# A new hand-written step order in four layers, and 46 products moved from GpSimd to VectorE

## The chip, the cores and the metric

The kernel runs on one core of a Trainium2 chip. The core has five engines that run their own instruction queues: TensorE (PE in the rows; PEld is its loading of weights), VectorE (DVE), ScalarE (ACT), GpSimd (POOL) and SyncE (SP, which here issues the loads from memory). The metric is the device time of one launch in microseconds (us).

## What is computed

A transformer of two blocks in float32, on 256 positions of 1024 features. The first block has an even layer (three kinds of gated attention on compressed, selected and windowed keys, plus differential attention) and an odd layer (block attention of 16 heads), each followed by an MLP. The second block has two equal layers without an MLP; each mixes three branches, gates them and projects the result:

```python
for layer in range(DEPTH):                    # second block, DEPTH = 2
    h = rms_norm_2(x, norm_g[layer])
    cols = split_columns(h @ w_in[layer])
    y_gdn = gdn_branch(cols, ...)             # gated delta rule, both directions, chunks of 64
    y_mla = mla_branch(cols, positions, ...)  # latent attention, 6 heads
    y_rwkv = rwkv7_branch(cols, ...)          # RWKV-7 recurrence, both directions
    mix = jnp.concatenate([y_gdn, y_mla, y_rwkv], axis=-1) * jax.nn.silu(cols['gate'])
    x = x + mix @ w_out[layer]
return rms_norm_2(x, final_norm_g)
```

Inside `gdn_branch`, with `cum` the running sum of the log decay of a chunk:

```python
d_incl = jnp.exp(jnp.where(incl, cum[..., :, None] - cum[..., None, :], -jnp.inf))
a_mat = beta[..., :, None] * jnp.einsum('nhcid,nhcjd->nhcij', k, k) * d_strict
sol = lax.linalg.triangular_solve(a_mat, rhs, lower=True, unit_diagonal=True)
```

## The kernel before

The program is first recorded and then laid out. Every operation of a layer is noted in a list (class `Order`), with the tiles that it reads and writes; when the list is complete, `Order.plan` lays it out once, at build time, into one fixed instruction list for each engine. It takes at each moment the ready operation with the smallest number in the list, within a window of 600 entries, and gives tiles their places in four arenas: `sb` (working tiles), `wt` (raw weights), `fr` (split weights and activations) and `ps` (PSUM banks). All instructions are issued by one helper, so they all carry line 614, `put`; rows are told apart by engine, operation, tile and shape.

Each layer is cut into parts, and each part into steps (a generator that yields after each). A string, `ORDER`, names one step after the other:

```python
def weave(self, order):
    for word in order.split():
        n, _, steps = word.partition("*")
        ...
        for _ in range(int(steps or 1)):
            if self.step(parts[n]):
                ended.add(n)
```

So `ORDER` sets the numbers in the list, and with them the priorities and, where several operations are ready, the order of the instructions on each engine.

A product with weights is done in three matmuls on split numbers (`mm3`): ScalarE copies the raw weights to the rounded type (the CAST `fr<-wt`), VectorE subtracts that copy from the raw weights (the weight subtraction, TENSOR_TENSOR `fr<-wt,fr`, most of them 128x1024), and TensorE multiplies high and low parts. Matmuls with output 128x512 on `fr` tiles are called wide below. A matmul on `sb` tiles in plain float32 stands as one row in the program's order and as two records in the trace.

The parts that matter here:

- Even layer E: `attn0` to `attn3`, `diff0`, `diff1` (differential attention), `cmpk` and `comp` (the compressed branch; its second step holds a softmax on VectorE and ScalarE, two transposes, and four products of 128x256), `out_a` (output projection of the first six feature tiles; needs `comp` and `diff0`), `out_b` (of the last two, 24 wide matmuls; needs `diff1`).
- Odd layer O: `proj0` to `proj3` (projections of four head groups), `attn0` to `attn3` (scores, softmax on ScalarE, transposes, products), `out_a`, `out_b`.
- A layer of the second block, S0 and S1: `gdn_proj`, `gdn_prep`, `gdn_inv` (the triangular inverse by small matmuls of 32x32 and 64x64), `gdn_uw`, `gdn_steps`, `gdn_end`; the same for `rwkv_proj`, `rwkv_prep`, `rwkv_inv`, `rwkv_mats`, `rwkv_steps` (the chain of 64x64 matmuls over the chunks), `rwkv_end`; `mla_proj`, `mla_attend`, `mla_end`; `gates` (column blocks of the gate projection); `out_a` (output projection of the feature tiles of gdn and mla), `out_b` (of rwkv's two tiles, 24 wide matmuls).

In `gdn_prep` (L1837) a copy of 128x48 takes the running sums out of PSUM, copies of 64x12 and 128x12 turn them round, and then 14 products of 128x384 on `gu`, `m`, `E` and `EN` (L1887 to L1906) and exponentials on ScalarE make the matrices to be inverted. In `gdn_end` two products of 128x384 (L2043) and in `rwkv_end` six of 128x256 and one of 128x512 (L2356 to L2363) make factors for the results. All these products name GpSimd as their engine; without a name `mul`, `add` and `sub` go to VectorE. GpSimd's other work is memsets, small DMAs of weights, `rstd_pool`, a product in `cmpk` and copies for `mla_proj`.

Of the kernel before, what the change touches and what calls it, by code (L numbers as in the profile page):

```python
# [1504 lines left out]
class Second(Layer):  # L1505
# [41 lines left out]
    def start(self):  # L1547
# [29 lines left out]
        "gdn_proj*10 rwkv_proj gdn_proj*4 rwkv_proj gdn_proj*2 rwkv_proj*2 gdn_prep*3 rwkv_proj gdn_prep*3 rwkv_proj "  # L1577
        "gdn_inv*2 rwkv_proj gdn_inv*2 rwkv_proj gdn_inv rwkv_proj*3 gdn_inv*6 rwkv_proj*2 gdn_inv*2 rwkv_proj "
        "gdn_inv*6 rwkv_proj gdn_inv*2 rwkv_proj gdn_inv rwkv_proj gdn_inv*3 rwkv_proj gdn_inv*5 rwkv_prep gdn_inv*3 "
        "rwkv_prep gdn_inv*6 rwkv_prep*4 gdn_inv gdn_uw rwkv_prep gdn_uw*3 rwkv_prep*2 gdn_uw*2 rwkv_inv*2 gdn_uw "  # L1580
        "rwkv_inv gdn_uw rwkv_inv*4 gdn_uw rwkv_inv gdn_uw rwkv_inv*11 gdn_uw rwkv_inv*2 gdn_steps rwkv_inv gdn_steps "
# [1033 lines left out]
```

## Time and profile before

| | |
|---|---|
| median of 3 runs | 1231.8 us (1231.16 to 1233.77) |
| the profiled execution | 1228.06 us |
| its span, first to last instruction | 1226.3 us |
| busy: TensorE | 1073.2 us (88% of the span) |
| busy: VectorE | 832.9 us (68%) |
| busy: ScalarE | 577.1 us (47%) |
| busy: GpSimd | 75.7 us (6%) |

The stages of the span, by the first and last instructions of their parts: E from 0 to 158.2, its MLP to 339.8, O to 460.0, its MLP to 641.7, S0 to 927.4, S1 to 1214.7, then the final norm. Busy is the time in which an engine executes an instruction; a share over the whole span mixes stages that have different limits.

### The profile page before, as it was taken

How to read it: one execution, taken by the hardware profiler on the slowest of the kernel's cores; microseconds unless marked ns; L12 is line 12 of the kernel's file. 1: busy time of each engine (PE TensorE's matmuls, PEld its weight loads, DVE VectorE, ACT ScalarE, POOL GpSimd, SP SyncE). 2: the span in 40 equal slices, each digit the busy share in tenths (PEclk: the TensorE clock that was granted, in tenths of full speed). 3: DMA queues.
4: the chain of work that ended last, by engine and by line, in shares of the span. 5: the costliest groups of instructions: out<-in, count | busy, mean ns of one | idle time of the engine just before them, and what ended most of it. 6: DMA issues, size and time to landing. Idle time of an engine off the chain costs nothing. (4 is left out here: it accounts for less than half of the span.)

```text
span 1226.3 us, 22320 instructions
## 1 busy us (share of the span) xinstructions
PE 1073.2 (88%) x8969; PEld 950.9 (78%) x8969; DVE 832.9 (68%) x1757; ACT 577.1 (47%) x1069; POOL 75.7 (6%) x150
## 2 busy tenths in 40 slices
PE   8999899999998999999997974489899895768895
PEld 7887699999897979999986873478568784657663
DVE  5556775545565566555488899962877889788445
ACT  4565454444436555444354543226564453332751
POOL 0000000000000000000001310002200310001200
PEclk9999899999998999999998885699899797678797
DMA  9930375565542454675671410142214342102110
GB/s 265 275 106 21 118 222 174 177 200 195 174 148 82 143 172 139 222 224 174 210 247 36 132 44 1 51 117 84 70 41 127 86 117 73 36 13 90 51 50 35
DMA packets 129682, 151.51 MB, mean 124 GB/s; under 512 B 15979, under 2 KB 111338, under 8 KB 129578
## 3 DMA queue, kind: packets, MB, share of 16 engines
q1 hardware_dynamic: 128745, 147.89, 38.7%
q0 software_dynamic: 832, 2.20, 0.7%
q8 instruction: 70, 1.15, 0.4%
q14 instruction: 35, 0.28, 0.1%
HBM read 147.42 MB, written 1.07 MB: 121 GB/s over the span
## 5 line engine op out<-in xcount | busy, mean ns | idle before, releaser
L614 PE MATMUL ps<-fr 128*128 128x256 f32 (+3 forms) x5112 | 788.1, 315 | 23.2 <-DVE fr L614 9.2
L614 PEld LDWEIGHTS ps<-fr 128*128 128x128 f32 (+1 forms) x5112 | 714.4, 194 | 83.6 <-DVE fr L614 14.4
L614 PE MATMUL ps<-sb 64*64 64x64 f32 (+14 forms) x3857 | 309.3, 286 | 118.3 <-DVE sb L614 83.3
L614 PEld LDWEIGHTS ps<-sb 64*64 64x64 f32 (+5 forms) x3857 | 241.1, 171 | 179.8 <-DVE sb L614 77.3
L614 DVE TENSOR_TENSOR fr<-wt,fr 128x1024 fp32r<-128x1024 f32 (+4 forms) x269 | 314.7, 1202 | 55.4 <-ACT fr L614 54.8
L614 ACT CAST fr<-wt 128x1024 fp32r<-128x1024 f32 (+4 forms) x269 | 263.0, 1022 | 80.7 <-DMA wt<-in_mlp_w 25.6
L614 ACT ACTIVATE sb<-sb 128x256 f32<-128x256 f32 (+8 forms) x347 | 163.3, 504 | 209.4 <-DVE sb L614 187.2
L614 DVE TENSOR_TENSOR sb<-ps,sb 128x256 f32<-128x256 f32 (+7 forms) x169 | 85.8, 517 | 171.5 <-ACT sb L614 90.0
L614 ACT ACTIVATE sb<-ps 128x384 f32<-128x384 f32 (+7 forms) x166 | 77.3, 475 | 228.2 <-PE ps L614 207.3
L614 DVE TENSOR_TENSOR sb<-sb 128x256 f32<-128x256 f32 (+24 forms) x436 | 146.1, 348 | 10.9 <-POOL sb L614 4.2
L614 DVE SCALAR_TENSOR_TENSOR sb<-sb 128x256 f32<-128x256 f32 (+8 forms) x228 | 88.8, 407 | 20.6 <-ACT sb L614 17.0
L614 DVE TENSOR_TENSOR sb<-sb,ps 128x512 f32<-128x512 f32 (+3 forms) x82 | 46.7, 582 | 31.9 <-PE ps L614 31.5
L614 POOL TENSOR_TENSOR sb<-sb 128x384 f32<-128x384 f32 (+4 forms) x55 | 52.8, 980 | 171.3 <-PE ps L614 97.3
L614 ACT ACTIVATE sb<-ps,sb 128x256 f32<-128x256 f32 (+3 forms) x70 | 34.8, 542 | 47.7 <-PE ps L614 45.7
L614 DVE TENSOR_TENSOR fr<-sb,fr 128x512 fp32r<-128x512 f32 (+1 forms) x38 | 24.7, 649 | 21.5 <-ACT fr L614 21.3
L614 ACT CAST fr<-sb 128x512 fp32r<-128x512 f32 x32 | 19.9, 621 | 32.4 <-DVE sb L614 32.4
L614 DVE COPY sb<-ps 128x384 f32<-128x384 f32 (+9 forms) x45 | 21.3, 478 | 19.7 <-PE ps L614 19.2
L614 POOL MEMSET sb<- 128x2 f32 (+3 forms) x59 | 5.7, 140 | 463.6 <-DVE sb L614 286.8
L614 DVE TENSOR_SCALAR sb<-sb 128x2 f32<-128x2 f32 (+15 forms) x119 | 26.2, 234 | 4.8 <-POOL sb L614 2.0
L614 DVE CUSTOM_DVE_ANT_0 sb<-ps,sb 128x128 f32<-128x128 f32 (+1 forms) x80 | 24.6, 352 | 6.7 <-PE ps L614 3.5
L614 POOL TENSOR_SCALAR sb<-sb 128x2 f32<-128x2 f32 (+1 forms) x8 | 2.5, 312 | 416.9 <-DVE sb L614 416.9
L614 ACT ACTIVATE fr<-ps,sb 128x256 fp32r<-128x256 f32 x52 | 19.8, 488 | 11.5 <-PE ps L614 10.8
(30 smaller groups left out, 162.8 us busy)
## 6 DMA issues: line engine op xcount, KB each, us to landing
wt<-in_mlp_w SPq DMA_DIRECT2D x128, 512.0 KB
wt<-in_w_in SPq DMA_DIRECT2D x38, 512.0 KB
wt<-in_od_w_in SPq DMA_DIRECT2D x24, 512.0 KB
wt<-in_w_out SPq DMA_DIRECT2D x16, 512.0 KB
wt<-in_ev_w_in SPq DMA_DIRECT2D x14, 512.0 KB
wt<-in_ev_w_in SPq DMA_DIRECT2D x16, 256.0 KB
wt<-in_ev_w_out SPq DMA_DIRECT2D x8, 512.0 KB
...
```

What stands on the lines that cost most here:

```text
L614: fn(*a, **k)
```

## The change

The strings `ORDER` of E, O, S0 and S1 are written anew; the steps and what they compute are the same, and each step is still named as often. In S0 and S1 the 46 products named above (23 in each layer) lose their engine's name and go to VectorE. The diff, with one line of each pair of strings; the strings go on behind the dots:

```diff
@@ class Even, ORDER @@
-        "dp1 attn1 dp1 cmpk dp1 attn2 dp0 cmpk diff1*2 dp0 attn1 attn3 diff1 attn3 diff1 attn1 diff1 attn3 diff1 cmpk "
-        "diff1*2 attn3 diff1 attn1 diff1 cmpk dp0 cmpk attn3 cmpk*2 dp0 cmpk comp dp0 out_b dp0 diff0 comp diff0*4 "
-        "out_b diff0*4 out_b diff0 comp out_a*10")
+        "attn1 diff1 cmpk*2 diff0 cmpk attn3 attn2 attn3 diff1 diff0 comp diff0*6 comp diff0 comp diff0 out_a out_b "
+        "out_a*3 out_b*2 out_a*6")
...
@@ class Odd, ORDER @@
-        "proj0*9 proj1*2 attn0 proj1*2 attn0 proj1 attn0 proj1*2 attn0 proj1*2 attn0 proj2 attn0 proj2 attn1 proj2*2 "
+        "proj1*6 proj0*6 proj2 proj0*3 proj1 attn0 proj1 proj2 attn0 proj2 proj3*2 proj1 proj2*3 proj3 attn1 proj3*3 "
...
@@ class Second, ORDER, second string (S1) @@
-        "mla_attend*2 rwkv_steps*2 mla_attend mla_end rwkv_steps mla_end rwkv_steps out_a*2 rwkv_end*2 out_a*3 "
-        "rwkv_end out_a*3 rwkv_end out_b*3 out_a*2")
+        "rwkv_steps*3 mla_attend*2 rwkv_end mla_attend*3 mla_end*2 rwkv_end out_a*3 rwkv_end out_a*3 rwkv_end out_b "
+        "out_a out_b*2 out_a*3")
...
@@ gdn_prep @@
-                self.mul(gu, b6(gd), bc6("inc" + "fb"[d]), nc.gpsimd)
+                self.mul(gu, b6(gd), bc6("inc" + "fb"[d]))
...
-                self.add(m, b6(cd), bc6("m" + "fb"[d]), nc.gpsimd)
+                self.add(m, b6(cd), bc6("m" + "fb"[d]))
...
-                    self.mul(E, E, b6(sb[:, t, 0]), nc.gpsimd)
+                    self.mul(E, E, b6(sb[:, t, 0]))
...
-                    self.sub(m, b6(cd), bc6("mn"), nc.gpsimd)
+                    self.sub(m, b6(cd), bc6("mn"))
...
-                    self.mul(EN, EN, b6(sb[:, t, 1]), nc.gpsimd)
+                    self.mul(EN, EN, b6(sb[:, t, 1]))
@@ gdn_end @@
-                     gr[:, None, None, :].to_broadcast([128, 3, 2, 64]), nc.gpsimd)
+                     gr[:, None, None, :].to_broadcast([128, 3, 2, 64]))
@@ rwkv_end @@
-            self.mul(G[:, t], sg[t], row("rwkv_ln_g_2"), nc.gpsimd)
+            self.mul(G[:, t], sg[t], row("rwkv_ln_g_2"))
...
-            self.add(B[:, t], B[:, t], row("rwkv_ln_b_2"), nc.gpsimd)
-            self.mul(B[:, t], B[:, t], sg[t], nc.gpsimd)
+            self.add(B[:, t], B[:, t], row("rwkv_ln_b_2"))
+            self.mul(B[:, t], B[:, t], sg[t])
```

**Place 1: TensorE at the end of E.** Before, from the transposes of `out_b`'s input, the two of `comp`'s second step and three of `diff0` (the nine of 128x128), over `comp`'s four products (128x256) and three more of `diff0` to the 24 wide matmuls of `out_b`:

```order
L614 MATMUL ps<-sb 128x128 x9
L614 MATMUL ps<-sb 128x256 x4
L614 MATMUL ps<-sb 128x128 x3
L614 MATMUL ps<-fr 128x512 x24
L614 MATMUL ps<-sb 128x128 x3
```

And of the changed kernel, up to `comp`'s four products and what follows them:

```order
L614 MATMUL ps<-fr 128x512 x4
L614 MATMUL ps<-sb 128x128 x3
L614 MATMUL ps<-fr 128x512 x3
L614 MATMUL ps<-sb 128x128
L614 MATMUL ps<-fr 128x512 x2
L614 MATMUL ps<-sb 128x128 x2
L614 MATMUL ps<-fr 128x512
L614 MATMUL ps<-sb 128x128 x2
L614 MATMUL ps<-fr 128x512 x2
L614 MATMUL ps<-sb 128x128 x3
L614 MATMUL ps<-sb 128x256 x4
L614 MATMUL ps<-fr 128x512 x12
```

17 of `out_b`'s wide matmuls (these 12, and five in the rows just ahead) and the transposes of `diff0` have moved from behind `comp`'s products to ahead of them; the other 7 stand among the 12 behind them.

In O the same can be said in words: before, four groups of scores are followed directly by the first six transposes of `attn0`; now 72 matmuls of 128x256, which belong to `proj3`, stand between scores of `attn2` and those transposes.

**Place 2: the front of S1, VectorE and TensorE.** VectorE before, around the copy of 128x48 in `gdn_prep`:

```order
L614 SCALAR_TENSOR_TENSOR sb<-sb 128x24 x2
L614 COPY sb<-ps 128x48
L614 TENSOR_TENSOR sb<-sb 128x24
L614 COPY sb<-sb 64x2x6 x4
L614 COPY sb<-sb 128x12 x2
L614 TENSOR_TENSOR sb<-ps,sb 128x384
L614 TENSOR_TENSOR fr<-wt,fr 128x1024 x4
```

VectorE of the changed kernel there:

```order
L614 SCALAR_TENSOR_TENSOR sb<-sb 128x24 x2
L614 TENSOR_TENSOR sb<-sb 128x384 x4
L614 COPY sb<-ps 128x48
L614 TENSOR_TENSOR sb<-sb 128x24
L614 TENSOR_TENSOR sb<-sb 128x384
L614 COPY sb<-sb 64x2x6 x4
L614 COPY sb<-sb 128x12
L614 TENSOR_TENSOR sb<-sb 128x384
L614 COPY sb<-sb 128x12
L614 TENSOR_TENSOR sb<-ps,sb 128x384
L614 TENSOR_TENSOR fr<-wt,fr 128x1024 x4
```

Four of the moved products (`sb<-sb 128x384`) stand ahead of the 128x48 copy and two among the copies behind it; the other eight follow later. TensorE in the same layer, where the 32x32 matmuls of `gdn_inv`'s last stage stand, before:

```order
L614 MATMUL ps<-fr 128x256 x46
L614 MATMUL ps<-sb 32x32 x96
L614 MATMUL ps<-sb 128x128 x7
L614 MATMUL ps<-fr 128x256 x4
L614 MATMUL ps<-sb 64x64 x12
```

And of the changed kernel:

```order
L614 MATMUL ps<-fr 128x256 x48
L614 MATMUL ps<-sb 32x32 x48
L614 MATMUL ps<-sb 128x128 x4
L614 MATMUL ps<-sb 32x32 x48
L614 MATMUL ps<-sb 128x2 x4
L614 MATMUL ps<-sb 64x64 x152
```

The four of 128x128 that now stand between the two halves are `rwkv_prep`'s, which VectorE scales next; they were the first four of the seven behind all 96.

**Place 3: TensorE at the end of S1.** The last steps of `rwkv_steps` (64x64), the wide matmuls of `out_a`, the four transposes of `out_b`'s input (128x128) and its 24 wide matmuls, before:

```order
L614 MATMUL ps<-sb 64x256 x3
L614 MATMUL ps<-sb 64x64 x8
L614 MATMUL ps<-fr 128x512 x30
L614 MATMUL ps<-sb 64x64 x16
L614 MATMUL ps<-fr 128x512 x36
L614 MATMUL ps<-sb 128x128 x4
L614 MATMUL ps<-fr 128x512 x24
```

And of the changed kernel (`mla_attend`'s last products are the 64x256):

```order
L614 MATMUL ps<-sb 64x64 x8
L614 MATMUL ps<-sb 128x128 x4
L614 MATMUL ps<-sb 64x64 x8
L614 MATMUL ps<-sb 64x256 x4
L614 MATMUL ps<-fr 128x512 x51
L614 MATMUL ps<-sb 128x128
L614 MATMUL ps<-fr 128x512
L614 MATMUL ps<-sb 128x128 x3
L614 MATMUL ps<-fr 128x512 x38
```

The 30 wide matmuls have gone from the middle of the 64x64 chain to behind it, so that 51 instead of 36 stand between the chain and the transposes; 10 of `out_a` and the 24 of `out_b`, among the last 38 with four more, follow them.

## Rows read from the trace of the kernel before

**Rows 1.** The page: the span, and each engine's busy time, share and instructions.
```profile
span 1226.3 us, 22320 instructions
...
PE 1073.2 (88%) x8969; PEld 950.9 (78%) x8969; DVE 832.9 (68%) x1757; ACT 577.1 (47%) x1069; POOL 75.7 (6%) x150
```
**Rows 2.** Windows by stage: length, busy PE, PEld, DVE, ACT, POOL, clock, DMA share, GB/s.
```profile
0.00:158.20 158.20, 142.75 (x1041) 126.03 (x1042) 98.43 (x268) 85.90 (x209) 5.05 (x12) 0.95 0.55 162
339.80:460.00 120.20, 115.73 (x870) 104.66 (x869) 71.31 (x151) 67.02 (x151) 0.89 (x2) 0.97 0.40 132
...
641.70:927.40 285.70, 221.34 (x2366) 191.09 (x2365) 226.75 (x553) 129.44 (x253) 33.75 (x66) 0.83 0.24 69
927.40:1214.70 287.30, 230.23 (x2362) 197.17 (x2360) 217.95 (x536) 122.96 (x242) 32.32 (x47) 0.82 0.22 63
```
**Rows 3.** Windows of three stretches: the end of E, O, the front of S0.
```profile
118.00:134.00 16.00, 10.94 (x64) 8.80 (x65) 14.75 (x49) 9.43 (x27) 1.05 (x1) 0.57 0.40 129
380.00:390.00 10.00, 6.54 (x29) 4.76 (x29) 6.91 (x29) 9.91 (x31) 0.00 (x0) 0.66 0.43 136
720.00:800.00 80.00, 38.98 (x818) 35.99 (x818) 77.13 (x207) 25.45 (x41) 0.52 (x1) 0.62 0.13 35
```
**Rows 4.** Timeline of TensorE: start, length, what, [idle before it <-releaser].
```profile
127.08 1.33 PE L614 MATMUL ps<-sb 128*128 128x128 f32 x5 [3.95 <-DVE sb L614]
129.11 4.21 PE L614 MATMUL ps<-sb 128*128 128x256 f32 x10 [0.70 <-DVE sb L614]
...
383.54 5.37 PE L614 MATMUL ps<-sb 128*128 128x128 f32 x20 [3.43 <-ACT sb L614]
...
806.31 3.59 PE L614 MATMUL ps<-fr 128*128 128x320 f32 x13 [0.65 <-DVE sb L614]
...
1048.73 4.22 PE L614 MATMUL ps<-sb 32*32 32x32 f32 x57 [0.19 <-ACT sb L614]
...
1191.30 1.08 PE L614 MATMUL ps<-sb 128*64 128x64 f32 x16 [0.48 <-ACT sb L614]
...
1194.30 8.37 PE L614 MATMUL ps<-fr 128*128 128x512 f32 x34 [0.34 <-DVE fr L614]
1204.60 0.88 PE L614 MATMUL ps<-sb 128*128 128x128 f32 x4 [1.94 <-DVE sb L614]
1206.17 8.57 PE L614 MATMUL ps<-fr 128*128 128x512 f32 x24 [0.69 <-ACT fr L614]
```
**Rows 5.** Timeline of VectorE, behind the inversion in S1.
```profile
1052.36 0.87 DVE L614 SCALAR_TENSOR_TENSOR sb<-sb,ps 128x256 f32<-128x256 f32 x2 [6.28 <-PE ps L614]
```
**Rows 6.** Groups by shape, GpSimd: count | busy, mean ns | idle before.
```profile
L614 POOL TENSOR_TENSOR sb<-sb 128x384 f32<-128x384 f32 x32 | 32.1, 1026 | 150.3 <-PE ps L614 77.1 <-DVE sb L614 57.4 <-ACT sb L614 15.7
```
**Rows 7.** Groups by shape, VectorE, 929 to 1215 us (S1).
```profile
L614 DVE TENSOR_TENSOR sb<-sb,ps 128x384 f32<-128x384 f32 x15 | 7.8, 547 | 3.7 <-PE ps L614 3.6
L614 DVE TENSOR_TENSOR sb<-sb 128x256 f32<-128x256 f32 x23 | 8.8, 421 | 0.2
```
**Rows 8.** Groups by shape, VectorE, 956.3 to 968.1 us.
```profile
L614 DVE TENSOR_TENSOR fr<-wt,fr 128x1024 fp32r<-128x1024 f32 x4 | 6.5, 1691 | 0.0
L614 DVE COPY sb<-sb 64x12 f32<-64x12 f32 x4 | 2.5, 692 | 0.0
L614 DVE TENSOR_TENSOR sb<-ps,sb 128x384 f32<-128x384 f32 x1 | 0.6, 558 | 0.0
L614 DVE COPY sb<-sb 128x12 f32<-128x12 f32 x2 | 0.2, 168 | 0.0
L614 DVE COPY sb<-ps 128x48 f32<-128x48 f32 x1 | 0.2, 207 | 2.8 <-PE ps L614 2.8
```
**Rows 9.** The page's costliest groups: the weight subtractions of the whole kernel.
```profile
L614 DVE TENSOR_TENSOR fr<-wt,fr 128x1024 fp32r<-128x1024 f32 (+4 forms) x269 | 314.7, 1202 | 55.4 <-ACT fr L614 54.8
```
**Rows 10.** Groups by shape, VectorE, 674 to 690 us (S0).
```profile
L614 DVE TENSOR_TENSOR fr<-wt,fr 128x1024 fp32r<-128x1024 f32 x6 | 8.3, 1428 | 0.7 <-ACT fr L614 0.7
L614 DVE COPY sb<-sb 64x12 f32<-64x12 f32 x4 | 1.7, 469 | 0.0
```

More of the change, by code (lines that the diff above doesn't have):

```diff
@@ L1441 @@
     ORDER = (
[4 rows of a table removed]
+        "proj1*6 proj0*6 proj2 proj0*3 proj1 attn0 proj1 proj2 attn0 proj2 proj3*2 proj1 proj2*3 proj3 attn1 proj3*3 "
+        "proj2 attn0*2 attn1*2 attn0*2 proj2*2 attn1*3 attn2*4 proj3*2 attn2 proj3 attn3*3 attn2 attn3 out_a attn3*2 "
+        "out_b*2 out_a*5 out_b out_a*3")
     def run(self):
@@ L1576 @@
     ORDER = (
[L1577 to L1581, printed above, removed]
@@ L1587 @@
-        "mla_proj gdn_end rwkv_end mla_proj mla_attend*6 rwkv_end mla_attend*6 gdn_end*2 mla_attend*4 rwkv_end*2 "
-        "out_b mla_end out_b mla_end out_a out_b out_a*9",
-        "gdn_proj*16 gdn_prep*2 gates gdn_prep gates*2 gdn_prep*2 gates gdn_prep gdn_inv gates rwkv_proj gdn_inv*2 "
-        "rwkv_proj gdn_inv*3 rwkv_proj gdn_inv*2 rwkv_proj*4 gdn_inv rwkv_proj gdn_inv rwkv_proj gdn_inv*10 "
-        "rwkv_proj*5 gdn_inv rwkv_proj*3 gdn_inv rwkv_proj gdn_inv*17 rwkv_prep gdn_inv rwkv_prep*4 gdn_uw rwkv_prep "
@@ L1592 @@
-        "gdn_uw rwkv_prep gdn_uw rwkv_prep gdn_uw rwkv_prep gdn_uw*2 rwkv_inv gdn_uw*3 rwkv_inv*2 gdn_uw*2 gdn_steps "
-        "rwkv_inv*2 gdn_steps rwkv_inv*5 gates rwkv_inv*4 gdn_steps rwkv_inv gates rwkv_inv gates rwkv_inv*3 "
-        "gdn_steps*3 gates rwkv_inv gdn_steps rwkv_inv gdn_steps gates*3 rwkv_inv rwkv_mats gdn_steps*2 rwkv_mats "
-        "rwkv_inv rwkv_mats*3 rwkv_inv rwkv_mats rwkv_inv*8 gdn_steps rwkv_inv rwkv_mats gdn_end mla_proj rwkv_inv "
-        "rwkv_mats*3 mla_proj rwkv_inv*4 gdn_end mla_proj rwkv_mats mla_proj*4 rwkv_steps*2 mla_proj rwkv_steps "
@@ new lines @@
+        "gdn_inv*3 rwkv_proj gdn_inv*6 rwkv_proj gdn_inv*7 rwkv_proj gdn_inv*5 rwkv_proj*3 gdn_inv*2 rwkv_proj "
+        "gdn_inv rwkv_prep*4 gdn_inv*6 rwkv_prep gdn_inv*2 rwkv_prep gdn_inv*2 rwkv_prep gdn_uw*3 rwkv_prep*2 "
+        "rwkv_inv gdn_uw rwkv_inv*17 gdn_uw*4 rwkv_inv*2 gdn_uw rwkv_inv gdn_uw*2 rwkv_inv gdn_steps*2 rwkv_inv "
+        "gdn_steps rwkv_inv gdn_steps rwkv_inv gdn_steps rwkv_inv gdn_steps gates gdn_steps*2 rwkv_inv rwkv_mats "
+        "gdn_steps gates rwkv_mats rwkv_inv*5 rwkv_mats*2 rwkv_inv gates rwkv_mats*2 gates*2 gdn_steps rwkv_mats*2 "
@@ new lines @@
+        "rwkv_inv gates rwkv_inv gdn_steps rwkv_mats gates rwkv_inv gates rwkv_inv rwkv_mats gates rwkv_inv rwkv_mats "
+        "rwkv_steps mla_proj gates rwkv_steps mla_proj rwkv_steps*2 mla_proj rwkv_steps*2 mla_proj rwkv_steps*2 gates "
+        "rwkv_steps mla_proj rwkv_steps mla_proj*3 rwkv_steps mla_proj*2 gates rwkv_steps gdn_end mla_proj "
+        "mla_attend*2 rwkv_end mla_attend*4 rwkv_end mla_attend*2 rwkv_end mla_attend*4 rwkv_end mla_attend gdn_end*2 "
+        "mla_attend*3 out_b mla_end out_b mla_end out_a*8 out_b out_a*2",
@@ new lines @@
+        "gdn_proj*16 gdn_prep*2 gates gdn_prep gates*2 gdn_prep*2 gates gdn_prep gdn_inv gates rwkv_proj gdn_inv*2 "
+        "rwkv_proj gdn_inv*4 rwkv_proj gdn_inv*3 rwkv_proj gdn_inv*4 rwkv_proj gdn_inv rwkv_proj gdn_inv rwkv_proj*2 "
+        "gdn_inv rwkv_proj gdn_inv rwkv_proj*2 gdn_inv*4 rwkv_proj gdn_inv rwkv_proj*2 gdn_inv*2 rwkv_proj gdn_inv "
+        "rwkv_proj gdn_inv rwkv_proj*2 gdn_inv*7 rwkv_prep gdn_inv rwkv_prep gdn_inv rwkv_prep*2 gdn_inv*4 "
+        "rwkv_prep*5 gdn_uw*6 rwkv_inv gdn_uw*2 rwkv_inv*2 gdn_uw rwkv_inv*2 gdn_uw rwkv_inv*8 gdn_uw gdn_steps gates "
@@ new lines @@
+        "rwkv_inv*3 gdn_steps rwkv_inv*4 gdn_steps gates gdn_steps*2 gates rwkv_inv gates gdn_steps*3 gates rwkv_inv "
+        "gates rwkv_inv rwkv_mats gdn_steps*2 rwkv_inv rwkv_mats*4 gates rwkv_inv*2 gdn_steps rwkv_inv*6 rwkv_mats "
+        "gdn_end rwkv_mats mla_proj rwkv_inv rwkv_mats*3 rwkv_inv mla_proj rwkv_inv*2 gdn_end rwkv_inv mla_proj*6 "
+        "rwkv_mats mla_proj rwkv_inv mla_proj*2 rwkv_steps*2 mla_attend rwkv_steps mla_attend rwkv_steps mla_attend*2 "
+        "rwkv_steps*2 mla_attend*3 rwkv_steps mla_attend rwkv_steps mla_attend*2 gdn_end rwkv_steps mla_attend "
```

11 lines of the change are left out of this document (3 added, 8 removed), and 8 rows, old and new, of the table ORDER.

## The prediction

> **What bounds the kernel now.** I read the page first, then the windows cut at the six stages, then the tensor engine's timeline at its longest waits, then the groups by shape of the vector engine and GpSimd. The page says that TensorE is busy for 1073.2 of 1226.3 us, so no more than 153 us of the span is its idle time [rows 1]. The windows say where that idle time lies: 15.5 us in the Even layer (158.20 less 142.75), 4.5 in the Odd layer, 64 and 57 in the two layers of the second block, S0 and S1 [rows 2]; the two MLP stages have next to none, and the change does not touch them. In S0 and S1 a second loss comes on top: the granted clock averages 0.83 and 0.82, so part of the matmuls run at 1.2 GHz instead of 2.4 [rows 2]. What TensorE waits for there is VectorE. From 720 to 800 us VectorE is busy for 77.13 of 80 us, TensorE for 38.98 at a mean clock of 0.62 [rows 3]. So E and O are limited by TensorE and its single waits, the front of S0 and S1 by VectorE's queue, and the end of each layer by a chain that hands work between the engines.
>
> A new order can therefore gain in two ways only: by putting ready matmuls into a wait of TensorE, or by making VectorE reach the head of a chain earlier. Moving GpSimd's products onto VectorE costs in the very place where VectorE is full, so the two halves of the change pull against each other.
>
> **The Even layer.** Before, TensorE waits 3.95 us for the transposes of the compressed branch's softmax and 0.70 us for its products (`comp`, second step) [rows 4]. 17 of the 24 wide matmuls of `out_b` and the last transposes of `diff0`, which stood behind the products before, now stand ahead of them, and they need only `diff1` and weights that were loaded long since. At 0.246 us for one wide matmul (8.37 us for 34) [rows 4] the 17 are 4.2 us, nearly as long as the two waits, 4.65. The stretch around it ran at a clock of 0.57, with 10.94 us of TensorE work in 16 us [rows 3]; if the clock stayed up, up to (1 - 0.57) x 10.94 = 4.7 us more would come back. Against this, VectorE is busy for 14.75 of those 16 us [rows 3], and what is late on it stays late. I take **-4 us**, between -9.3 (waits and clock) and +2 (the wait moves to the output projection `out_a`, which needs `comp` and has only 7 matmuls of `out_b` left for cover).
>
> **The Odd layer.** Before, the first transposes of `attn0` follow directly on four groups of scores and wait 3.43 us for ScalarE's softmax [rows 4]; nothing else is queued. Now 72 matmuls of 128x256, most of `proj3`'s, stand between, and more score groups are computed ahead. The window from 380 to 390 us has TensorE at 6.54 us with a clock of 0.66 [rows 3], so up to 3.4 us more was lost to the clock. I take **-5**, between -6.8 and 0. What could be late instead is the load of `proj3`'s weights; the layer moves only 132 GB/s, less than E's 162 [rows 2], so there is room.
>
> **The 46 moved products.** Per layer 14 products of 128x384 in `gdn_prep`, 2 in `gdn_end`, 6 of 128x256 and one of 128x512 in `rwkv_end`. On GpSimd a 128x384 took 1.03 us [rows 6]. On VectorE 15 products of 128x384 with an operand in PSUM are busy for 7.8 us, 0.52 each, and 23 of 128x256 in SBUF for 8.8 us, 0.38 each [rows 7]; the 128x512 scales to 0.69. That makes 14 x 0.52 = 7.3 us in `gdn_prep` and 2 x 0.52 + 6 x 0.38 + 0.69 = 4.0 us at the ends, 22.6 us for both layers. I price one by its busy time, since the next instruction starts before the duration shown has ended: by mean durations, 547 and 421 ns [rows 7], the 46 would be 24.0. The Trainium skill ("VectorE: DVE Perf Modes", section The DRAIN you can't avoid) says that the next VectorE operation does not start until the pipe is empty, though it allows an earlier start in some cases; by that rule the whole duration is the price, and the sum below would be 1.4 us longer. The trace shows the earlier start.
>
> What comes back is the slowing that GpSimd causes. Under seven and then three GpSimd products in S1, four copies of 64x12 take 692 ns where a 128x12 copy beside them takes 168, and four weight subtractions take 1691 ns [rows 8] against 1202 on average over the kernel [rows 9]: 4 x 0.52 + 4 x 0.49 = 4.1 us. In S0 it is 6 x 0.23 + 4 x 0.30 = 2.6 us [rows 10]. An operation that reads PSUM is not slowed: 558 ns in the same stretch [rows 8]. The Trainium skill ("GPSIMD Engine Reference", section Specifications) says that GpSimd contends with VectorE instructions that have two SBUF inputs or run in a two-port mode; by that rule just the copies and subtractions gain, and the trace agrees. If every VectorE instruction gained 41%, as the subtractions do, the relief over about 12 us of GpSimd work would be 4.9 instead of 4.1 us and the sum 0.8 us shorter.
>
> So `gdn_prep` costs 7.3 - 4.1 = 3.2 us net in S1. Of this the wait of 2.8 us before the 128x48 copy [rows 8] can hide most, since six of the moved products now stand in the order ahead of that copy; I take +1 (0.4 to 3.2). In S0 it is 7.3 - 2.6 = 4.7, with a shorter wait to hide in: +2.5 (0 to 4.7). At the ends nobody waits for the moved products until the last step of `rwkv_end`, and VectorE has gaps there: +1 in each layer (0 to 4.0).
>
> **S0 besides.** One column block of `gates`, 24 wide matmuls that stood wholly behind `gdn_steps` and were broken by waits, now partly fills the front. 13 of them took 3.59 us [rows 4], so 24 are 6.6 us; as only matmuls that fall into a real wait count, I take -3 (0 to -6.6). S0 in sum: 2.5 + 1 - 3 = **+0.5**.
>
> **S1 besides.** After the inversion's 192 records of 32x32, VectorE waits 6.28 us for eight matmuls of `rwkv_prep` [rows 5], which stand behind all of them on TensorE (the last 57 pieces, these eight included, run for 4.22 us [rows 4]). Now they stand behind the first half, and three weight subtractions of 1.2 us can fill what remains. VectorE bounds this stretch, so the wait is worth its length at most: -4 (0 to -6.3). At the end, `out_b` waits 1.94 and 0.69 us for `rwkv_end`, and its 24 wide matmuls then need 8.57 us, 0.357 each instead of 0.246 [rows 4]: 2.6 us of waits and 2.7 of slow clock. Between the last `rwkv_steps` and `out_b` stood 36 wide matmuls, 8.9 us; now there are 51, 12.5 us, and 30 of these came out of the middle of the `rwkv_steps` chain, which so ends earlier. `rwkv_end` takes about 12 us, from the last step's end near 1192.4 to 1204.60 [rows 4], and is then covered. I take -5 (0 to -6.5). S1 in sum: 1 + 1 - 4 - 5 = **-7**.
>
> **The sum.** -4 - 5 + 0.5 - 7 = -15.5 us. The profiled execution took 1228.06 us, the span of 1226.3 and 1.8 around it, so 1212.6; the median of the runs shown is 3.7 us above it, which gives 1216.
>
> **Rivals.** First, *VectorE keeps the second block's time*: what a filled wait gives to TensorE there is spent waiting for the same VectorE queue, 226.75 of 285.70 us busy in S0 [rows 2]. S0 and S1 come out at 0 together and only E and O pay: 1231.8 - 9 = 1223. For it speaks that the vector work ahead of the end of the second inversion is nearly the same in both orders; against it, that the wait of 6.28 us is VectorE's own. Second, *the new order moves waits without removing them*: each filled wait opens another, and the moved products cancel the rest: 1232, no change. Third, on the other side, *the moved products fall where nothing covers them*: the full 22.6 us less the relief of 6.7 is +16, and with E and O at half their gain, -4.5, the time is 1243. It decides once more than 9 us, what E and O give, are neither covered nor returned; the 77.13 of 80 us busy speaks for it, the 2.8 us and 6.28 us of VectorE's waiting against it.
>
> **How the numbers follow.** A measurement of this kernel tells 0.2% from no change, 2.5 us. Chances: the forecast 0.50, the first rival 0.24, the second 0.08, the third 0.18. The first two are faster: 0.74. The prediction is the likeliest case, 1216. Its own bounds, with all S1 and O terms at their best, reach to 1200; upwards the range takes in the first and second rivals and the near part of the third: 1236. Case three beyond that and a still better E leave 2 in 10 out.
>
> **What would show it.** In the changed profile the Odd layer should last 115 us instead of 120, with no wait over 1 us before `attn0`'s transposes; the wait of 3.95 us before `comp` should be under 1; VectorE should not wait over 2 us after the S1 inversion; `out_b` in S1 should start without a wait. GpSimd's busy time should fall from 75.7 [rows 1] to about 30, VectorE's rise from 832.9 by some 16 us. The weight subtractions of S1 should be back at 1.2 us. I am wrong if S0 or S1 grows by more than 4 us, if a load of weights ends a long wait of TensorE in O, or if the clock in E's last 40 us stays at half.

## The result and the profile after

The changed kernel takes 1199.28 us (median of 4 runs, 1197.06 to 1202.72) against 1231.48 before; the ratio is 0.9739, with a 95% interval of 0.9707 to 0.9770. It gained 32 us where 15.5 were forecast, and lies 0.7 us below the lower end of the range.

The page of the changed kernel, its span and busy times, answers to [rows 1]:

```profile
span 1195.6 us, 22343 instructions
...
PE 1059.7 (89%) x8969; PEld 945.4 (79%) x8969; DVE 835.7 (70%) x1803; ACT 575.1 (48%) x1069; POOL 29.4 (2%) x104
```

GpSimd fell to 29.4 us, as forecast. VectorE rose by 2.8 us only, not by 16. The windows by stage (E, O, S0, S1; columns as in [rows 2]; like every window below, from one profiled execution):

```profile
0.00:145.20 145.20, 136.34 (x1041) 122.06 (x1042) 97.65 (x268) 85.37 (x209) 5.20 (x12) 0.99 0.58 177
326.80:441.00 114.20, 113.61 (x870) 104.68 (x869) 72.49 (x152) 67.72 (x152) 0.89 (x2) 1.00 0.44 140
622.60:916.10 293.50, 228.69 (x2367) 196.79 (x2365) 228.85 (x577) 129.55 (x253) 10.91 (x43) 0.80 0.23 66
916.10:1184.60 268.50, 217.91 (x2362) 189.92 (x2360) 221.52 (x559) 123.65 (x243) 8.90 (x24) 0.83 0.23 70
```

E is 13.0 us shorter, O 6.0, S1 18.8; S0 is 7.8 longer. The two MLPs are unchanged. The idle time of TensorE in E fell from 15.5 to 8.9 us, and the granted clock rose from 0.95 to 0.99: about half of E's gain is waits, half is clock. In S1 TensorE's idle time fell by 6.5 us and its busy time by 12.3.

The timeline of TensorE at the places of [rows 4]: the end of E, the first transposes of `attn0` in O, and the end of S1.

```profile
113.47 2.99 PE L614 MATMUL ps<-sb 64*128 64x16 f32 x24 [0.71 <-DVE sb L614]
...
123.12 2.56 PE L614 MATMUL ps<-sb 128*128 128x128 f32 x14
...
378.87 4.19 PE L614 MATMUL ps<-sb 64*128 64x128 f32 x44
382.99 5.70 PE L614 MATMUL ps<-fr 128*128 128x256 f32 x44
388.85 3.62 PE L614 MATMUL ps<-fr 128*128 128x256 f32 x28 [0.15 <-DVE fr L614]
392.31 3.00 PE L614 MATMUL ps<-sb 128*128 128x128 f32 x28
...
1163.27 11.94 PE L614 MATMUL ps<-fr 128*128 128x512 f32 x51
1175.05 0.31 PE L614 MATMUL ps<-sb 128*128 128x128 f32 x1
...
1175.68 8.97 PE L614 MATMUL ps<-fr 128*128 128x512 f32 x38
```

The rows of 128x128 are the transposes, and none of them has a bracket: the waits of 3.95 us before `comp`, 3.43 before `attn0` (between its scores and its transposes stand the matmuls of `proj3`) and 1.94 before `out_b` are gone, and the last 38 wide matmuls take 0.236 us each instead of 0.357. VectorE at the two places of S1 that answer to [rows 5] and [rows 8]; the three groups are from 944 to 955 us, the last two rows from the timeline behind the inversion:

```profile
L614 DVE TENSOR_TENSOR fr<-wt,fr 128x1024 fp32r<-128x1024 f32 x3 | 3.5, 1217 | 0.0
L614 DVE TENSOR_TENSOR sb<-sb 128x384 f32<-128x384 f32 x6 | 3.1, 552 | 0.0
...
L614 DVE COPY sb<-sb 64x12 f32<-64x12 f32 x4 | 0.5, 164 | 0.0
...
1035.26 3.49 DVE L614 TENSOR_TENSOR fr<-wt,fr 128x1024 fp32r<-128x1024 f32 x3
1038.67 0.87 DVE L614 SCALAR_TENSOR_TENSOR sb<-sb,ps 128x256 f32<-128x256 f32 x2
```

Three weight subtractions stand where VectorE waited 6.28 us, the subtractions are back at 1.2 us, and the 64x12 copies at 0.16.

### The profile page after: what moved, and what is told of

It is laid out like the page before. It is cut to its first block, busy times and chain, and to the rows that moved or that the text cites. A ratio compares the mean times of both kernels' runs of the same rounds, so it can differ in the third digit from the quotient of the medians.

```text
span 1195.6 us, 22343 instructions
## 1 busy us (share of the span) xinstructions
PE 1059.7 (89%) x8969; PEld 945.4 (79%) x8969; DVE 835.7 (70%) x1803; ACT 575.1 (48%) x1069; POOL 29.4 (2%) x104
## 5 line engine op out<-in xcount | busy, mean ns | idle before, releaser
L614 PE MATMUL ps<-fr 128*128 128x256 f32 (+3 forms) x5112 | 790.5, 316 | 28.8 <-DVE fr L614 11.8
L614 PE MATMUL ps<-sb 64*64 64x64 f32 (+13 forms) x3857 | 293.4, 281 | 96.2 <-DVE sb L614 61.9
L614 PEld LDWEIGHTS ps<-sb 64*64 64x64 f32 (+5 forms) x3857 | 232.9, 169 | 149.3 <-DVE sb L614 53.0
L614 DVE TENSOR_TENSOR fr<-wt,fr 128x1024 fp32r<-128x1024 f32 (+4 forms) x269 | 308.4, 1186 | 29.4 <-ACT fr L614 28.9
L614 ACT ACTIVATE sb<-sb 128x256 f32<-128x256 f32 (+9 forms) x347 | 162.5, 504 | 213.1 <-DVE sb L614 195.6
L614 ACT ACTIVATE sb<-ps 128x512 f32<-128x512 f32 (+7 forms) x166 | 76.9, 475 | 224.0 <-PE ps L614 204.7
L614 DVE TENSOR_TENSOR sb<-sb 128x256 f32<-128x256 f32 (+22 forms) x482 | 163.0, 356 | 12.9 <-PE ps L614 4.1
L614 DVE TENSOR_SCALAR sb<-sb 128x256 f32<-128x256 f32 (+15 forms) x119 | 25.7, 231 | 5.4 <-ACT sb L614 2.2
L614 DVE SCALAR_TENSOR_TENSOR fr<-ps,sb,fr 128x256 fp32r<-128x256 f32 x52 | 21.1, 477 | 5.1 <-ACT fr L614 3.0
L614 DVE SCALAR_TENSOR_TENSOR sb<-ps,sb 128x256 f32<-128x256 f32 (+1 forms) x24 | 12.3, 530 | 17.4 <-PE ps L614 17.4
L614 DVE STREAM_TRANSPOSE sb<-sb 128x1024 f32<-128x1024 f32 x12 | 17.5, 1468 | 3.0 <-ACT sb L614 2.8
```

The costliest lines, as they stand in the source:

```text
L614: fn(*a, **k)
```

## The experiments

One thing said ahead of the prediction was too simple. `Order.plan` is not run once: it is run for 36 packings (rules for where a tile goes in its arena), and of the plans that find room (21 in the kernel before, 19 in the changed one) the one that is cheapest by its own costs is kept. A new string in one layer can so change the packing, and with it the order of instructions, in the whole program. Therefore one family of runs holds the packing, and another freezes the whole plan: the recorded order and places are written into the kernel, and only the named thing differs. Ratios are to the kernel before, timed on the same chip; medians in different rows can come from different chips, and where the two disagree the ratio is the safer one.

| run | median us | ratio, 95% |
|---|---|---|
| before_fixed_packing | 1241.91 | 1.0061 (1.0042 to 1.0080) |
| products_only | 1239.11 | 1.0046 (1.0029 to 1.0063) |
| orders_only | 1213.10 | 0.9833 (0.9807 to 0.9860) |
| s0_old_order | 1208.13 | 0.9780 (0.9747 to 0.9812) |
| after_plan_products_back | 1208.05 | 0.9792 (0.9767 to 0.9816) |
| before_plan_products_moved | 1234.56 | 1.0017 (0.9999 to 1.0036) |
| after_plan_rwkv_end_back | 1203.27 | 0.9759 (0.9740 to 0.9778) |
| before_plan_filled_E | 1228.20 | 0.9963 (0.9946 to 0.9980) |
| e_order_alone | 1229.19 | 0.9970 (0.9954 to 0.9986) |
| before_plan_tail_moved | 1233.68 | 1.0008 (0.9991 to 1.0024) |
| before_plan_tail_both_queues | 1232.95 | 0.9999 (0.9985 to 1.0013) |
| tail_signal_ahead | 1232.18 | 0.9984 (0.9968 to 1.0000) |
| tail_all_queues | 1226.14 | 0.9946 (0.9924 to 0.9967) |
| after_other_packing | 1209.72 | 0.9815 (0.9791 to 0.9838) |
| s1_old_other_packing | 1225.83 | 0.9948 (0.9928 to 0.9967) |
| after_plan_filled_S | 1195.13 | 0.9696 (0.9681 to 0.9710) |
| after_plan_filled_late | 1196.99 | 0.9715 (0.9694 to 0.9737) |

**Orders and products apart, packing held.** Four kernels, all with this edit:

```diff
-        self.packings = [(f, l, s, b) for b in (0, 1) for s in (0, 2, 4) for l in (300, 500, 900) for f in (False, True)]
+        self.packings = [(True, 900, 4, 0)]
```

before_fixed_packing is the old kernel so; products_only has the products' part of the diff, orders_only the strings, s0_old_order is the changed kernel with the old string of S0.

> The kernel before, but planned with the one packing of buffers that the plan of the changed kernel took, instead of the cheapest of 24. Theory A (each layer's time comes from its own step order and from the products; packing is noise): 1231 us, between 1226 and 1236, E at 158 us. Rival B (a good part of the gain is the packing that came with the new strings): 1221 or less, E at 152 or less.

> Old orders in all four layers, the 46 products on VectorE, packing held at that of the changed kernel. Theory A: E and O as in the old-order run beside it; S0 and S1 longer by what gdn_prep and the ends pay, 2 to 7 us together, so that much above the old-order run. Rival C (the products cause all of S0's loss of 7.6 us): S0 alone 7 to 8 us longer, the whole 8 to 12 above it. Rival D (the products help, by ending GpSimd's slowing of VectorE): below it by 2 or more.

> New orders in all four layers, the 46 products left on GpSimd, packing held at that of the changed kernel. Theory A: 2 to 7 us below the changed kernel, 1192 to 1197. Rival C (the products cause all of S0's loss): S0 at 286 us, 1190 or less. Rival D (the products help): above 1201, with S0 or S1 longer than in the changed kernel.

> The changed kernel with S0's old order, the rest as it is, packing held. Theory A (the new order of S0 is itself worse, by about half of the 7.6 us, the products the other half): S0 at 288 to 291 us, the whole at 1193 to 1197. Rival C (the products alone): S0 stays at 293 and the time at 1199. Rival E (the order alone): S0 at 286, the time at 1192 or less.

Rival B is out: with the packing of the changed kernel the old one is 0.6% slower, and E takes 166 us instead of 158. But that packing hardly matters, as theory A has it, is wrong too: the difference is larger than most terms of the prediction. The new strings alone took 28.8 us off it (1241.91 to 1213.10): E from 166.2 to 146.2 us, O from 119.8 to 114.3. The products alone took 2.8 by the medians, which is not clear of the scatter (the two intervals overlap). On top of the new orders they take 14 more by the medians, 11.6 by the ratios (orders_only against the changed kernel, both with this packing, but planned anew). Theory A, which had them cost 2 to 7 us, falls; rival D stands with the new orders and is open with the old ones. For S0, rival C had the stage right and the time wrong: with its old order it lasted 293.6 us, the same as with the new one, and S1 behind it, whose plan shifted, 277.9 instead of 268.5. With the old kernel in this packing S0 is as long:

```profile
649.10:944.40 295.30, 226.65 (x2366) 195.88 (x2365) 230.26 (x553) 129.63 (x253) 34.37 (x66) 0.82 0.24 68
```

**The products in a frozen plan.** The plan no longer answers to the move, so only the products differ. In the changed kernel's plan all 46 go back, or only the 14 of `rwkv_end`; in the old kernel's plan the 46 move.

```diff
 def flush(self):
-        preds = self.graph()
...
+        log, at = json.loads(zlib.decompress(base64.b64decode(PLAN)))
+        best = 0.0, log, {k: v for k, v in at}, {}
```

```diff
-            self.mul(G[:, t], sg[t], row("rwkv_ln_g_2"))
+            self.mul(G[:, t], sg[t], row("rwkv_ln_g_2"), nc.gpsimd)
...
-            self.mul(B[:, t], B[:, t], sg[t])
+            self.mul(B[:, t], B[:, t], sg[t], nc.gpsimd)
```

> The changed kernel's own plan, frozen: every instruction in the same order and every buffer in the same place, only the 46 products issued on GpSimd again. Theory A (the prediction's price: the products cost 2 to 7 us net on VectorE): 1192 to 1197. Rival D (they help: on GpSimd each takes twice as long on a chain that S0 and S1 wait for, and slows VectorE): 1202 or more, with the loss in gdn_prep and in the ends, and no other stage moved.

> The kernel before with its own plan frozen, only the 46 products issued on VectorE at their places in the plan. Theory A: 2 to 7 us above the kernel before. Rival D: 3 or more below it, half of it in each of S0 and S1.

> The changed kernel's own plan, frozen; only the seven products of rwkv_end in each layer are issued on GpSimd again, the other 32 stay on VectorE. Theory J (GpSimd's products slow the small operations of mla_proj's norm on VectorE, on which TensorE waits): 4 to 7 us above the changed kernel, 1203 to 1206, with mla_proj's end 2.5 to 4 us later in each of S0 and S1 and nothing ahead of it moved. Rival K (the products of gdn_prep make the 8.8 us): within 2 us of the changed kernel.

With the products back the changed kernel loses 8.8 us by the medians (6.5 by the ratios to before); every one of its five runs, 1204.71 to 1208.94, is longer than every run of the changed kernel. In the old plan the move changes nothing that can be told, -0.01% to +0.36%, so rival D falls there; why it gives nothing in that plan was not tried. With `rwkv_end` alone back it is 4.0 by the medians, but some of the runs overlap, and the two intervals do too; what carries the verdict is the trace. VectorE in S1 at the norm of `mla_proj`, a chain of operations on 128x4 values, in the changed kernel from 1125.2 to 1128.3 us:

```profile
L614 DVE SCALAR_TENSOR_TENSOR sb<-sb 128x4 f32<-128x4 f32 x6 | 1.0, 162 | 0.2
L614 DVE TENSOR_TENSOR sb<-sb 128x4 f32<-128x4 f32 x4 | 0.7, 162 | 0.1
```

The same ten operations and two conversions in after_plan_products_back, from 1128.5 to 1135.05 us, then what GpSimd does meanwhile, and one of them in the timeline:

```profile
L978 DVE SCALAR_TENSOR_TENSOR sb<-sb 128x4 f32<-128x4 f32 x6 | 2.6, 433 | 0.2
L978 DVE TENSOR_TENSOR sb<-sb 128x4 f32<-128x4 f32 x4 | 1.5, 369 | 0.1
...
L978 POOL TENSOR_TENSOR sb<-sb 128x256 f32<-128x256 f32 x6 | 4.5, 765 | 13.1 <-DVE sb L978 12.8
L978 POOL TENSOR_TENSOR sb<-sb 128x512 f32<-128x512 f32 x1 | 1.2, 1230 | 0.0
...
1130.62 0.89 DVE L978 SCALAR_TENSOR_TENSOR sb<-sb 128x4 f32<-128x4 f32 x1
```

An operation on four values per partition lasts 0.89 us instead of 0.16 while a GpSimd product runs: it does not get slower by a share of its own work, it waits, for up to about the length of a product (0.77 us in the mean). The Trainium skill ("SBUF — State Buffer", section SBUF: two separate sides) says that the port pair of the two engines is locked for a whole instruction, so that the later one is blocked; the rows agree. The chain takes 6.5 us instead of 3.0, and TensorE waits for it: the stretch from the end of `rwkv_mats` to the end of `mla_proj` in S1 is 29.5 us in the changed kernel, 33.4 with all products back, and 33.6 with those of `rwkv_end` alone. So theory J holds for S1. For S0 it does not: there this stretch is 51.1, 53.6 and 51.3, and the loss came with the other products. The relief can be read from the pages too. This is VectorE's busy time with the products back, in the same plan; the changed kernel has 46 operations more and only 2.8 us more (835.7):

```profile
PE 1058.6 (88%) x8969; PEld 942.0 (78%) x8969; DVE 832.9 (69%) x1757; ACT 574.8 (48%) x1069; POOL 69.5 (6%) x150
```

**The clock in E.** Into the old kernel's frozen plan come 23 matmuls of 128x128 that write an unused PSUM bank and that nobody reads, 8 in the wait before `diff1`'s last step and 15 in the one before `comp`'s transposes. e_order_alone is the old kernel, planned with its own packing, with E's new string.

The 23 stand as negative entries in the frozen list; besides the list, one line of the program is new, which gives them something to read:

```diff
+        self.order.idle = self.ident
```

The wait before `diff1`'s last step, and the windows of 4 us behind it, in the old kernel (the clock is the third figure from the end):

```profile
111.02 0.33 PE L614 MATMUL ps<-sb 128*128 128x128 f32 x1 [1.97 <-DVE sb L614]
...
112.00:116.00 4.00, 3.75 (x21) 2.71 (x20) 2.63 (x4) 2.04 (x4) 0.00 (x0) 0.64 0.02 4
116.00:120.00 4.00, 3.48 (x44) 3.00 (x43) 2.60 (x8) 1.21 (x3) 2.25 (x3) 0.93 0.00 0
120.00:124.00 4.00, 3.13 (x20) 2.07 (x18) 4.00 (x16) 2.52 (x11) 0.00 (x0) 0.50 0.48 139
```

> The kernel before with its own plan frozen, with 8 and 15 matmuls of 128x128 that nobody reads put into two waits of TensorE at the end of E (before diff1's last step, before comp's transposes). No wait is taken away. Theory H (half of what E gains in the changed kernel is the clock that stays up): granted clock of E at 0.98 or more, E at 152 to 154 instead of 158.2, the time 4 to 6 below the kernel before. Rival I (only the waits count, the clock is a mark of them): E at 158 or more, the time unchanged or up to 1 us longer.

> The kernel before with E's new order alone; packing held at that of the kernel before. Theory H (E's own order gives its stage 13 us, half waits and half clock): E at 145 to 147, the time 9 to 14 below the kernel before, 1219 to 1224. Rival O (E's gain is half the packing's): E at 150 to 154, the time 4 to 8 below.

The windows of E from 105 to 140 us, of the old kernel and of the filled one, and two lines of the filled one's timeline (the fillers have line 769):

```profile
105.00:140.00 35.00, 27.41 (x162) 21.14 (x161) 24.72 (x72) 14.90 (x41) 2.25 (x3) 0.76 0.27 90
```

```profile
105.00:140.00 35.00, 32.15 (x218) 26.63 (x217) 25.25 (x71) 14.96 (x39) 2.25 (x3) 0.90 0.28 91
...
108.48 2.05 PE L769 MATMUL ps<-sb 128*128 128x128 f32 x16
...
122.69 4.88 PE L769 MATMUL ps<-sb 128*128 128x128 f32 x30
```

With no wait taken away the kernel is 0.37% faster (0.20 to 0.54), 4.5 us by the medians on one chip; the mean clock there is 0.90 instead of 0.76. Theory H stands in its mechanism: the time came as it said, and the clock, while E itself lasted 155.8 us in the profile where it had 152 to 154. Rival I falls. In the old kernel the clock fell to half twice, at 113 us, behind the wait before `diff1`, and again at 120 us, before the wait at `comp` had begun. Most of E's gain is still the order: E's new string alone made its stage 148.6 us, 9.6 shorter, between theory H (145 to 147) and rival O. But the kernel as a whole gained only 0.3%, less than either had, since S1, whose string is the old one there, was planned differently behind the earlier start and took 298.3 us instead of 287.3. The time of one layer alone says little of the whole here.

**The end of S1.** Four kernels in the old plan, each with one move more than the one ahead of it. On TensorE:

```
before:     ... rwkv_steps (9) | 30 wide of out_a | rwkv_steps (9, 10) | 36 wide | out_b
tail_moved: ... rwkv_steps (9) | rwkv_steps (9, 10) | 30 wide of out_a | 36 wide | out_b
```

In both_queues three additions of `out_a` also stand behind the start of `rwkv_end` on VectorE; in signal_ahead `rwkv_end`'s first copy is written ahead of the 30 matmuls in the program, with every engine's own order as it was; in all_queues the addition of the last group stands behind `rwkv_end`, and 10 of the wide matmuls behind `out_b`'s transposes.

> The kernel before with its own plan frozen, except that in S1 the 30 wide matmuls of out_a which stand between the parts of the last rwkv_steps stand behind them. Theory F (on TensorE's queue these matmuls hold up the chain, and the tail behind it has room for them): the chain ends 6 us earlier, the waits before out_b go, S1 at 281 and the time 6 us below the kernel before. Rival G (VectorE's rwkv_end bounds the tail wherever the matmuls stand): no change within 1 us.

> As the run before_plan_tail_moved, and on VectorE three additions of out_a's results (two of the 30 moved matmuls' groups and one of the next) also stand behind the first steps of rwkv_end instead of ahead of them. Theory F2 (the 6.9 us that the chain gained there were lost again in VectorE's queue, where rwkv_end's first copy stood behind two additions that waited for the moved matmuls): rwkv_end starts within 1 us of the chain's end, S1 at 281 to 283 and the time 4 to 6 below the kernel before. Rival G (rwkv_end and out_b take the time anyway): no change within 1 us.

> As before_plan_tail_both_queues, and rwkv_end's first copy on VectorE is written in the program ahead of the 30 wide matmuls instead of behind them; the order on each engine is the same as there. Theory N (there the copy waited 3.7 us after the chain's end for a signal of TensorE that came with the sixteenth wide matmul, and so the chain's gain was lost): the copy starts within 0.2 us of the chain's end, out_b's transposes 3 to 4 us earlier, and the time is 3 to 5 below the kernel before. Rival G (the end is bound by rwkv_end and out_b in any case): no change within 1 us.

> As tail_signal_ahead, and the addition of out_a's last group stands on VectorE behind rwkv_end and out_b's split instead of ahead of rwkv_end's last three steps; the last 10 wide matmuls of out_a stand behind out_b's transposes on TensorE, as in the changed kernel. Theory N2 (each of the runs before moved the wait to the next instruction in VectorE's queue, 5.0 us of it to this addition in the last): out_b's transposes start without a wait, S1 ends 4 to 6 us after less than before, at 280 to 282, and the time is 4 to 6 below the kernel before. Rival G (the end is bound by rwkv_end and out_b in any case): no change within 1 us.

In each run the chain's last matmuls ended 6 to 7 us earlier, counted from the start of S1, and only the last was faster clear of the scatter. So F, F2 and N each had the chain right and the time wrong. VectorE's timeline of tail_moved, from the end of the chain at 1188.2 us:

```profile
1191.85 0.69 DVE L978 TENSOR_TENSOR sb<-sb,ps 128x512 f32<-128x512 f32 x1 [5.49 <-PE ps L978]
1195.24 0.69 DVE L978 TENSOR_TENSOR sb<-sb,ps 128x512 f32<-128x512 f32 x1 [2.71 <-PE ps L978]
1195.85 0.68 DVE L978 COPY sb<-ps 128x512 f32<-128x512 f32 x1
```

The copy is ready at 1188.2, but two additions that wait for the moved matmuls stand ahead of it. In both_queues, where they do not (the chain's last matmuls on TensorE, then the copy on VectorE):

```profile
1191.64 1.08 PE L978 MATMUL ps<-sb 128*64 128x64 f32 x16 [0.48 <-ACT sb L978]
...
1196.40 0.69 DVE L978 COPY sb<-ps 128x512 f32<-128x512 f32 x1 [5.48 <-PE ps L978]
```

Its data are there at 1192.7; it is released 3.7 us later, by the profile when one of the wide matmuls behind ends. In signal_ahead, which differs in the writing alone (so that the release, and not the queues, made the difference), it starts 0.04 us after the chain's end at 1192.02, and the wait turns up at an addition of `out_a` that still stands ahead of `rwkv_end`'s last three steps:

```profile
1192.06 0.69 DVE L978 COPY sb<-ps 128x512 f32<-128x512 f32 x1 [1.84 <-PE ps L978]
...
1207.41 0.69 DVE L978 TENSOR_TENSOR sb<-sb,ps 128x512 f32<-128x512 f32 x1 [4.98 <-PE ps L978]
```

In all_queues it is gone as well, and TensorE runs from the chain to the end without a wait:

```profile
1188.34 13.17 PE L978 MATMUL ps<-fr 128*128 128x512 f32 x56
1201.35 0.60 PE L978 MATMUL ps<-sb 128*128 128x128 f32 x4
1201.70 8.00 PE L978 MATMUL ps<-fr 128*128 128x512 f32 x34
```

S1 is 279.6 us instead of 287.3, and the time 0.54% lower (0.33 to 0.76), 6.7 us, a little more than N2 had. N2 stands, G falls.

**S1's own order, and another packing.** after_other_packing is the changed source with the packing (True, 900, 2, 1); s1_old_other_packing has S1's old string besides.

> The changed kernel's source, planned with another of the 24 packings of buffers. Theory M (which plan the packing brings moves S0 and S1 by several us each, up and down, as it did in the kernel before): 1203 to 1215, E and O within 1.5 us of the changed kernel, S1 at 272 or more. Theory A (packing is noise): 1199 within 3.

> As after_other_packing, but with S1's old order. Everything ahead of S1 is the same there, instruction for instruction. Theory P (S1's own order gives what its stage gained, 10 us or more, mostly in the rwkv_steps chain): S1 at 286 to 290 against 277.5, the time at 1218 to 1222. Rival Q (most of S1's gain came from the products and the packing): S1 at 280 or less, the time within 3 us of after_other_packing.

The windows of S1, with the new string and with the old one, everything ahead of S1 being the same:

```profile
919.20:1196.70 277.50, 219.31 (x2363) 190.15 (x2361) 222.30 (x559) 123.82 (x243) 8.77 (x24) 0.83 0.22 65
```

```profile
918.40:1213.20 294.80, 232.08 (x2363) 198.05 (x2360) 224.23 (x559) 124.01 (x242) 8.97 (x24) 0.81 0.21 61
```

S1's order is worth 17.3 us with the products on VectorE in both, more than P had (294.8 where it had 286 to 290); P stands as to the size, and that it comes mostly from the chain of `rwkv_steps` is not shown by this run. M stands in its main point: with another packing the same source takes 1209.72 us, 10 more than with its own, of which S1 has 9.0 and E 5.0 (150.2 us, further off than expected).

**The clock in S0 and S1.** Fillers in the changed kernel's frozen plan, as negative entries in the list: 263 in after_plan_filled_S, 217 in after_plan_filled_late, which has the same ones in S1.

> The changed kernel's own plan, frozen, with 263 matmuls of 128x128 that nobody reads put into 31 waits of TensorE of 0.8 us or more in S0 and S1 (84 us of waits; where no PSUM bank is free, none). Theory H (the half clock that follows a wait makes the matmuls behind it take twice as long, and there they are on the path): granted clock of S0 and S1 at 0.9 or more and the time 6 to 15 below the changed kernel, 1184 to 1193. Rival L (in S0 and S1 VectorE's queue sets the time, and a faster TensorE waits longer): within 3 us of it, or longer by what the fillers hold up.

> As after_plan_filled_S, without the fillers in the first 110 us of S0 (217 instead of 263), where gdn_prep ended 3.7 us later with them. If the fillers cost that there: 1191 to 1193. If that was the run's own scatter: 1195 within 1.

The windows of S0 and S1 with all 263 fillers, and of S1 in after_plan_filled_late:

```profile
625.30:918.20 292.90, 248.50 (x2636) 215.73 (x2635) 228.38 (x577) 129.54 (x253) 10.91 (x43) 0.91 0.23 66
918.20:1182.40 264.20, 237.07 (x2619) 209.30 (x2616) 221.07 (x559) 123.76 (x243) 9.26 (x24) 0.92 0.25 71
...
918.50:1187.20 268.70, 243.25 (x2618) 214.68 (x2616) 221.48 (x559) 123.86 (x243) 8.93 (x24) 0.90 0.24 70
```

With all 263 it is the fastest of all, 1195.13 us, and its four runs lie within 0.44 us. The clock is at 0.91 and 0.92, and yet the gain is 4.2 us by the medians, less than theory H asked for, and the interval of its ratio just touches that of the changed kernel. By the windows S1 has 4.3 of it and S0 0.6, although S0's clock went from 0.80 to 0.91: TensorE's speed does not set that stage's time. But in after_plan_filled_late the same fillers left S1 at 268.7 us, where it was without any, so that S1's share is not shown. That run takes 1196.99 us, with runs up to 1202.00: the fillers in the front of S0 did not cost what was supposed.

## Why the prediction was right or wrong

**What bounds the kernel** was read rightly, and most of the signs that the prediction named came: the waits before `comp`, `attn0` and `out_b` and the one behind S1's inversion are gone, O lasts 114.2 us, the subtractions are back at 1.2 us, GpSimd is at 30. Two did not: VectorE's busy time rose by 2.8 us and not by 16, and S0 grew by 7.8 us in the profiles, more than the 4 that were to show that it is wrong. By stages -4 for E became -13.0, -5 for O -6.0, +0.5 for S0 +7.8 and -7 for S1 -18.8. The step behind the misses in E and S1 is that a new order gains "in two ways only", by filling a wait of TensorE or by bringing VectorE earlier to the head of a chain. The runs show two more ways. A clock that stays up gained 0.37% where no wait was taken away (before_plan_filled_E), and matmuls taken out of the middle of a chain on TensorE's own queue, with VectorE's queue turned round as well, gained 6.7 us (tail_all_queues).

**The Odd layer, -5:** 6.0 measured, within its bounds; 3.9 of it is TensorE's idle time and 2.1 its busy time, so the clock. The bound of 6.8 was too wide: it takes the 0.34 of clock that were lost from the whole window of 10 us and not, as in E, from TensorE's 6.54 us, which gives 2.2.

**The Even layer, -4: the term was mis-sized, 13.0.** It counted the two waits at `comp` and put the clock, up to 4.7, into the bound alone. The fillers show that the clock was worth 2.4 us (E's window, 158.2 to 155.8) to 4.5 us (the medians) by itself, and it was lost from 113 us on, ahead of the stretch that was read, behind a wait of 1.97 us before `diff1`'s last step that the argument did not contain. This wait and the two at `comp` come to 6.6 us, and E's idle time fell by as much; TensorE's busy time fell by 6.4, the clock. The step that failed is "nearly as long as the two waits": a new order of a whole layer was priced at the two places that the diff showed. The 13.0 hold for these two plans: E's string alone gave 9.6 us in the old kernel's packing and 20.0 in the changed one's.

**The moved products: the sign was wrong in the new order.** They were priced at +1 and +2.5 in `gdn_prep` and +1 at each end, in sum +5.5. In the old plan they cost -0.1 to 4.4 us, in the new one they give 6.5 to 8.8. The term that was mis-sized is the relief. It was read off the copies and subtractions in `gdn_prep` alone, 4.1 and 2.6 us, and put at nothing for the products at the ends, since "nobody waits for the moved products". Nobody does, but VectorE's small operations beside them are waited for, and these lost up to 0.7 us each to a GpSimd product. In the changed kernel's plan the 46 products, 22.6 us by the prediction's own prices, add only 2.8 us to VectorE's busy time, so that some 20 us of it came back instead of 6.7. This is why it did not rise by 16.

**S0, +0.5:** 7.8 longer in the profiles, but about half of that is the draw of the old profile. S0's instruction list is the same in six profiles of the old plan, [rows 2] and the five runs on it that left S0 alone, and lasts 285.7 to 292.4 us there, 289 in the middle, with VectorE's busy time within 0.5 us. The longest, in both_queues:

```profile
642.00:934.40 292.40, 228.13 (x2366) 196.73 (x2365) 226.68 (x554) 129.43 (x253) 33.65 (x66) 0.80 0.24 67
```

The granted clock is 0.80 in it and 0.83 in the shortest, that of [rows 2]. Against these six the changed S0 is 1 to 8 us longer, and against the old kernel in the same packing (295.3) it is 1.8 shorter; that the change itself made S0 longer is not shown. The term's -3 for the filled waits did not come: with the old string the stage lasted as long, and with the fillers too. That fits the first rival's mechanism, that VectorE keeps the time; in S0 it held as far as the runs tell.

**S1, -7: 18.8.** Counted from the start of S1, `gdn_prep` ended 1.3 us later, as forecast (+1). From there to the end of `rwkv_mats` 8.5 us were gained where -4 was taken for the wait behind the inversion; what makes up the rest was not tried. To the start of the `rwkv_steps` chain 1.6 were lost. The chain itself took 45.4 us before and 32.3 after, and what stands behind it 22.3 in both. The windows of the chain and of what is behind it, before and after:

```profile
1147.00:1192.40 45.40, 41.06 (x399) 29.36 (x398) 21.11 (x45) 31.47 (x79) 6.72 (x7) 0.88 0.13 50
1192.40:1214.70 22.30, 18.39 (x64) 13.40 (x64) 15.15 (x31) 4.96 (x7) 0.00 (x0) 0.85 0.00 1
```

```profile
1130.00:1162.30 32.30, 29.14 (x356) 22.08 (x357) 17.70 (x44) 28.04 (x75) 0.00 (x0) 0.86 0.20 66
1162.30:1184.60 22.30, 22.30 (x103) 17.40 (x100) 17.07 (x35) 6.66 (x9) 0.00 (x0) 1.00 0.00 1
```

The end was priced at -5, as waits and slow clock before and in `out_b`. These did go (TensorE is busy for all of the 22.3 us, at full clock), but the 30 matmuls that came out of the chain took their place, and so the gain is not there: the step that failed is that the end's gain was looked for behind the chain and the chain itself was given no term. In the old plan the same move made the chain 6.3 us shorter and the time 6.7, and it pays only when VectorE's queue is turned round as well. The other half of the chain's gain was not tried. By the matmuls in the windows `mla_attend` has 3.1 us less there, `mla_proj` 1.3 and TensorE's idle time 1.1; the granted clock, 0.88 before and 0.86 after, is not the cause.

**The sum and the range.** The terms were independent guesses about a plan that is drawn anew as a whole. With another packing the same source is 10 us slower, and S1 behind a changed S0 or E moved by 9 to 11 us. The range's lower end is not what its sentence says: S1 and O at their best take 7.2 us off 1216, which gives 1209, and with S0 at its best too 1202. All four layers at their best give 1197, which takes in what was measured.
